# RWKV-7 chunks without transitions of their own, on one Trainium2 core

## The chip, the cores and the metric

The kernel runs on one core of a Trainium2 chip, in one launch. The metric is device time in microseconds (us), the median of several runs. Below, PE is the matmul engine (TensorE), DVE is VectorE, ACT is ScalarE, POOL is GpSimd and SP issues most DMAs. All data are float32; the large projections split each operand into a high and a low part of a shorter float format and add three products of those.

## The reference, cut to what matters

A two-layer trunk step over 640 tokens (512 latent, 128 context). Layer 1 has, beside another mixer, a bidirectional RWKV-7 mixer: 8 heads of width 64, each with a 64x64 state that is updated token by token, forwards and backwards.

```
def rwkv_direction(r, w, kk, a, v, kt, s0, reverse):
    def step(state, inp):
        r_t, w_t, kk_t, a_t, v_t, k_t = inp
        sa = jnp.einsum('bhvk,bhk->bhv', state, -kk_t)
        state = (state * w_t[:, :, None, :] + sa[..., None] * (kk_t * a_t)[:, :, None, :]
                 + v_t[..., None] * k_t[:, :, None, :])
        return state, jnp.einsum('bhvk,bhk->bhv', state, r_t)
    ...
    s_fin, o = lax.scan(step, s0, xs, reverse=reverse)
```

The kernel computes this in chunks of 64 tokens. Inside a chunk the vectors `sa` (called U) solve a triangular system: U = X (A S + K V), where S is the state at the chunk's start, X the inverse of a unit triangle made from the chunk's keys, A the decayed keys and K V the part that the chunk's own values give. The next state is decay x (S + B' U + K' V).

## The kernel before, in words

The RWKV work is cut into 8 units: 4 pairs of heads times 2 directions (`t = 2 p + d`). A unit has 10 chunks of 64 tokens: 8 of the latent sequence, one after the other, and 2 of the context sequence. The two heads of a pair lie on partitions 0 to 63 and 64 to 127 (`HS`; `KS` is the crossed order). Each unit passes three stages, each a Python generator in `rwkv`:

- `stage_a` (L1396) loads five operand arrays through `load`, multiplies them with the decays into `ar` (right sides A and receptance R) and `bk` (left sides), and forms the Gram products `gram`, masked on DVE into `gx` (L1444). The transposed left sides go to `gx` as well, the transposed values to `UV`.
- `stage_b` (L1475) inverts the triangle: 15 small DVE steps on 16x16 blocks, a trip through DRAM, then block merges with 32x32 products in the PSUM tag `pw`. After that it forms, for all ten chunks of both heads, what no state is needed for: it copies A and K V into `az`, multiplies both with the inverse (L1561), and multiplies the result once more with the left sides (`back`, L1546), which makes of every chunk a 64x64 transition matrix (in `ar[..., 0]`), a corrected right side (`ar[..., 1]`) and an own contribution (`UV`).
- `stage_c` (L1572) walks over the chunks. One link per chunk: two products of each head add up in one PSUM tile `HN` (L1606 to L1609: own contribution, and transition times state), ACT scales head 0's half and DVE head 1's half into the next state `hst` (L1612, L1613). `outputs` (L1585) forms the outputs of four chunks at a time in the tag `pz` (tile `O`).

The order is not written out by hand. In round `t` of the loop at L1651, `in_turn` deals out steps (`yield`s) of three streams in proportion to the counts that it is given: one stream with `finish`, then `stage_c` of unit t-2, then `stage_a` of unit t; one with `stage_b` of unit t-1; one with `FILL[t]` steps of the other mixer and of the projections (tiles `g` and `m`). A list scheduler then sets the final order of each engine from the dependencies, free buffers and times that it assumes. Each engine takes its own list strictly in order. PSUM has two buffers for `pw` and one for `pz`.

Of the kernel before, what the change touches and what calls it, by code (L numbers as in the profile page):

```python
# [291 lines left out]
class Trunk:  # L292
# [821 lines left out]
    def inputs(self, p, mix):  # L1114
# [31 lines left out]
        nc.vector.tensor_tensor(bb, bb, kk, op=ALU.mult)  # L1146
# [3 lines left out]
        nc.sync.dma_start(self.sp[p, 1], r)  # L1150
# [200 lines left out]
    def rwkv(self, other, most, more):  # L1351
# [44 lines left out]
        def stage_a(t, u):  # L1396
# [21 lines left out]
            kk = cl(rev(load(p, 0)))  # L1418
            nc.vector.tensor_scalar(ar[:, :, 0, 0:1], kk[:, :, 0:1], -1.0, None, op0=ALU.mult)
            nc.vector.scalar_tensor_tensor(ar[:, :, 0, 1:], kk[:, :, 1:], -1.0, e[:, :, :L - 1], op0=ALU.mult, op1=ALU.mult)  # L1420
            nc.vector.tensor_tensor(ar[:, :, 1, :], cl(rev(load(p, 1))), e, op=ALU.mult)
# [5 lines left out]
            gx = op.tile([P, 2, NCH, 3, L], F32, tag="gx", bufs=2, name="gx")  # L1427
            gA = gx[:, :, :, 0]
            UV = op.tile([P, 2, NCH, L], F32, tag="UV", bufs=2, name="UV")
# [8 lines left out]
            for c0, n in groups:  # L1438
                pss = [self.pt(tag, [P, 4, 2, L], "gram") for tag in ("pg", "pz")]
                for i in range(n):  # L1440
                    for h, hs in enumerate(HS):
                        self.mm(pss[h][:, i], fl(bk[hs, c0 + i]), fl(ar[hs, c0 + i]))
                for h in range(2):
                    nc.vector.tensor_tensor(gx[:, h, c0:c0 + n, 0:2], pss[h][:, :n], mg[:, :n], op=ALU.mult)  # L1444
                    yield
            for h, hs in enumerate(HS):
                nc.sync.dma_start(scr[h], gA[hs, h])
# [10 lines left out]
            for c0, n in groups:  # L1458
                ps = self.pt("pg", [P, 4, 2, L])
                for i in range(n):  # L1460
                    self.tr(fl(ps[:, i]), fl(bk[:, c0 + i]), ident)
                nc.scalar.copy(gx[:, :, c0:c0 + n, 2, :].rearrange("p h c l -> p c h l"), ps[:, :n])
                yield
            for c0 in range(0, NCH, 5):
                ps = self.pt("pg", [P, 5, L])
                for i in range(5):
                    for h, hs in enumerate(HS):
                        self.mm(ps[KS[h], i, :], vs[hs, (c0 + i) * L:(c0 + i + 1) * L], ident[hs, hs])
                for h, ks in enumerate(KS):
                    nc.scalar.copy(UV[ks, h, c0:c0 + 5, :], ps[ks])  # L1470
                yield

        def stage_b(t, u):


            ar, gA, gx, UV, sd = [u[n] for n in ("ar", "gA", "gx", "UV", "sd")]
# [27 lines left out]
            az = op.tile([P, NCH, 2, L], F32, tag="az", name="az")  # L1504
            for c0, n in ((0, 8), (8, 2)):
                for j in range(2):
                    ps = self.pt("pw", [P, 8, L])
                    for i in range(n):
                        for h, hs in enumerate(HS):
                            if j == 0:  # L1510
                                self.mm(ps[hs, i, :], ar[hs, c0 + i, 0, :], ident[hs, hs])
                            else:
                                self.mm(ps[hs, i, :], gA[KS[h], h, c0 + i, :], UV[KS[h], h, c0 + i, :])
                    (nc.vector.tensor_copy if j else nc.scalar.copy)(az[:, c0:c0 + n, j, :], ps[:, :n])
                    yield
# [14 lines left out]
            for i in range(NCH):  # L1530
                for h in range(2):
                    self.mm(ps[R4[2 * h + 1], i, :], gA[R4[2 * h], h, i, 32:64], xp[R4[2 * h], i, :])
# [7 lines left out]
            for h in range(2):  # L1540
                r0, r1 = R4[2 * h], R4[2 * h + 1]
                nc.vector.tensor_copy(gA[r0, h, :, 32:64], ps[r0])
                nc.scalar.copy(gA[r0, h, :, 0:32], xt[r0])
                nc.scalar.copy(gA[r1, h, :, 32:64], xt[r1])
            yield
            wts = []  # L1546

            def back(w4, c0, n):
                cs = slice(c0, c0 + n)
                ps = self.pt("pw", [P, 4, 2, L])  # L1550
                for i in range(n):
                    for h, hs in enumerate(HS):
# [4 lines left out]
            for c0, n in groups:  # L1557
                ps = self.pt("pw", [P, 4, 2, L])
                for i in range(n):
                    for h, hs in enumerate(HS):  # L1560
                        self.mm(ps[hs, i], gA[hs, h, c0 + i, :], az[hs, c0 + i])  # L1561
                w4 = op.tile([P, 4, L], F32, tag="w4", bufs=2, name="w4")
                nc.scalar.copy(w4[:, :n], ps[:, :n, 0, :])
                for h, hs in enumerate(HS):
                    nc.scalar.copy(UV[hs, h, c0:c0 + n, :], ps[hs, :n, 1, :])
                wts.append((w4, c0, n))
                yield
                if c0:
                    back(*wts.pop(0))
                    yield  # L1570
            back(*wts.pop(0))

        def stage_c(t, u):


            p, d = divmod(t, 2)
            ar, gx, UV, dec = [u[n] for n in ("ar", "gx", "UV", "dec")]
# [7 lines left out]
            def outputs(c0, n):  # L1585
                O = self.pt("pz", [P, 4, L], "O")
                for i in range(n):
                    Hc = st[c0 + i]
                    if Hc is not None:
                        for h, hs in enumerate(HS):  # L1590
                            self.mm(O[hs, i, :], Hc[:, h, :], ar[:, c0 + i, 1, :], start=True, stop=False)
                    for h, hs in enumerate(HS):
                        self.mm(O[hs, i, :], UV[:, h, c0 + i, :], gx[:, h, c0 + i, 1, :], start=Hc is None, stop=True)
# [6 lines left out]
            for s, n in [(1, 0), (0, 0), (1, 1), (0, 1)] + [(1, n) for n in range(2, 8)]:  # L1600
                ch = n + ((2 if d else 0) if s else (0 if d else 8))
                Hc = st[ch] = H[s]
                if s == 0 or n < 7:
                    HN = self.pt("pz", [P, L], "HN")
                    for h, hs in enumerate(HS):
                        self.mm(HN[hs], gx[:, h, ch, 2, :], UV[:, h, ch, :], start=True, stop=Hc is None)  # L1606
                    if Hc is not None:
                        for h, hs in enumerate(HS):
# [47 lines left out]
        for t in range(11):  # L1656
# [70 lines left out]
```

## Time and profile before

| | us |
|---|---|
| median of 3 runs (lowest, highest) | 2183.33 (2182.89, 2183.53) |
| profiled execution, whole | 2182.15 |
| profiled execution, span from first to last instruction | 2180.4 |
| stretch with the RWKV units, from the span's start | about 1040 to 1665 |

The profile lists, for each engine, what it did and what ended its idle time. A matmul of the program in plain float32 appears as two records, a projection's as one. Records of PE overlap in time, so the pace of a kind of product is read from one start to the next and not from its duration. Forms such as 128*64 give the part of PE's array that a product uses (rows*columns); 128*128 is all of it.

### The profile page before, as it was taken

The numbers are of one execution on the slowest core, as the hardware profiler recorded it, in microseconds if no ns is written. First come the engines' busy times: TensorE is split into PE (matmuls) and PEld (weight loads), VectorE is DVE, ScalarE is ACT, GpSimd is POOL, SyncE is SP. The second block draws the span as 40 slices with busy tenths as digits, with TensorE's granted clock in tenths as the row PEclk, the third lists the DMA queues.
The fourth block names the chain that finished last, engine by engine and source line by source line (L and its number), as shares of the span: only waits on it lengthen the run. The fifth ranks groups of instructions, "written<-read, shape, count | busy, mean of one in ns | idle before, by whom it ended". The sixth has DMA issues, their size and how long they took to land.

```text
span 2180.4 us, 44790 instructions
## 1 busy us (share of the span) xinstructions
PE 2080.5 (95%) x18461; PEld 1895.1 (87%) x18461; DVE 1349.3 (62%) x3067; ACT 1018.6 (47%) x2072; POOL 0.2 (0%) x4
## 2 busy tenths in 40 slices
PE   7899989999999999999999999898989999999997
PEld 5896778888899999989888788786777999999997
DVE  3858686557636647746774755745567674574663
ACT  4645464455414515546655545544344552452551
POOL 0000000000000000000000000000000000000000
PEclk9899999999999999999999999998989999999999
DMA  7114420125525222332542242332312222222212
GB/s 295 60 46 151 141 66 25 44 99 205 205 86 183 67 79 78 109 106 72 167 117 81 74 118 83 97 100 84 94 31 61 76 70 78 78 66 81 74 62 89
DMA packets 138061, 212.50 MB, mean 97 GB/s; under 512 B 51456, under 2 KB 68736, under 8 KB 131712
## 3 DMA queue, kind: packets, MB, share of 16 engines
q1 hardware_dynamic: 131168, 205.56, 29.2%
q10 hardware_dynamic: 6688, 4.07, 0.6%
q8 instruction: 145, 2.38, 0.5%
q14 instruction: 60, 0.49, 0.1%
HBM read 187.49 MB, written 22.09 MB: 96 GB/s over the span
## 4 chain that ended last, share of the span: by engine, by line
PE 85%; DVE 7%; DMA 4%; ACT 3%; issue 1%; SPq 0%; ACTq 0%; DVEq 0%
PE e L331 46%; PE g L331 21%; PE m L331 5%; PE pw L331 4%; PE S L331 3%; PE m L334 2%; DMA wa<-in_adaw 1%; PE gram L331 1%; PE pg L331 1%; PE HN L331 1%; PE O L331 1%; DMA in<-sp 1%; DVE wl L578 0%; ACT pr L768 0%; PE pg L334 0%
## 5 line engine op out<-in xcount | busy, mean ns | idle before, releaser
L331 PE MATMUL e<-hi,wh 128*128 128x320 f32 (+1 forms) x2240 | 693.4, 312 | 3.2 <-ACT hi L511 1.8
L331 PE MATMUL e<-lo,wh 128*128 128x320 f32 (+1 forms) x2240 | 695.5, 311 | 0.1
L331 PE MATMUL e<-hi,wl 128*128 128x320 f32 (+1 forms) x2240 | 691.3, 310 | 2.1 <-DVE wl L578 2.1
L577 ACT CAST wh<-wr 128x512 fp32r<-128x512 f32 (+3 forms) x434 | 237.6, 586 | 519.8 <-PE e L331 385.2
L331 PEld LDWEIGHTS e<-hi,wh 128*128 128x128 f32 x2240 | 421.4, 189 | 19.6 <-ACT tg L965 7.5
L331 PEld LDWEIGHTS e<-hi,wl 128*128 128x128 f32 x2240 | 422.9, 189 | 8.6 <-DVE wl L578 3.6
L331 PEld LDWEIGHTS e<-lo,wh 128*128 128x128 f32 x2240 | 422.5, 189 | 1.3 <-DVE lo L513 1.3
L578 DVE TENSOR_TENSOR wl<-wr,wh 128x512 fp32r<-128x512 f32 (+3 forms) x434 | 267.7, 647 | 74.5 <-ACT wh L577 73.9
L331 PE MATMUL g<-hi,wh 128*128 128x320 f32 (+1 forms) x928 | 302.9, 327 | 3.9 <-DVE x L625 1.3
L331 PE MATMUL g<-lo,wh 128*128 128x320 f32 (+1 forms) x928 | 296.0, 319 | 1.3 <-DVE lo L475 1.3
L331 PE MATMUL g<-hi,wl 128*128 128x320 f32 (+1 forms) x928 | 296.2, 319 | 0.0
L331 PEld LDWEIGHTS g<-hi,wh 128*128 128x128 f32 x928 | 178.4, 193 | 14.2 <-issue 2.2
L331 PEld LDWEIGHTS g<-lo,wh 128*128 128x128 f32 x928 | 178.3, 192 | 5.4 <-DVE lo L475 1.8
L331 PEld LDWEIGHTS g<-hi,wl 128*128 128x128 f32 x928 | 178.3, 192 | 2.5 <-issue 1.0
L625 DVE SCALAR_TENSOR_TENSOR x<-e,mod,x 128x320 f32<-128x320 f32 x168 | 67.0, 437 | 139.6 <-PE e L331 139.4
L966 ACT ACTIVATE tu<-tu,bias 128x512 f32<-128x512 f32 (+1 forms) x176 | 88.6, 548 | 0.0
L553 DVE TENSOR_SCALAR bias<-e 128x2 f32<-128x2 f32 x95 | 15.2, 159 | 117.1 <-PE e L331 117.1
L768 ACT ACTIVATE pr<-S,nm 128x768 f32<-128x768 f32 (+1 forms) x80 | 63.7, 797 | 47.5 <-DVE nm L766 28.1
L766 DVE TENSOR_REDUCE nm<-S 128x1 f32<-128x768 f32 (+1 forms) x80 | 65.1, 820 | 17.5 <-PE S L331 16.9
L976 ACT ACTIVATE tg<-tg 128x640 f32<-128x640 f32 x44 | 32.5, 739 | 79.9 <-DVE tg L943 79.9
L554 DVE TENSOR_TENSOR tu<-e,rstd 128x320 f32<-128x320 f32 x86 | 41.8, 488 | 38.3 <-PE e L331 38.2
L331 PE MATMUL g<-wa,csT 128*32 128x512 f32 x352 | 49.5, 635 | 12.1 <-DMA wa<-in_adaw 12.0
(398 smaller groups left out, 2914.5 us busy)
## 6 DMA issues: line engine op xcount, KB each, us to landing
wa<-in_adaw SPq DMA_DIRECT2D x48, 1024.0 KB
wr<-in_wup SPq DMA_DIRECT2D x176, 256.0 KB
wr<-in_wod SPq DMA_DIRECT2D x70, 256.0 KB
wr<-in_wdn SPq DMA_DIRECT2D x64, 256.0 KB
in<-sp SPq DMA_DIRECT2D x42, 320.0 KB
wr<-in_wev SPq DMA_DIRECT2D x36, 256.0 KB
wr<-in_wdn SPq DMA_DIRECT2D x32, 192.0 KB
x<-in_xT SPq DMA_DIRECT2D x8, 320.0 KB
```

The costliest lines, as they stand in the source:

```text
L331: self.nc.tensor.matmul(out, lhsT, rhs, start=start, stop=stop)
L334: self.nc.tensor.transpose(out, in_, ident)
L553: nc.vector.tensor_scalar(bias, p1[:, HT:], scale, None, op0=ALU.mult)
L554: nc.vector.tensor_tensor(t[:, :HT], p0, self.rs[:, :HT], op=ALU.mult)
L577: nc.scalar.copy(wh[:, a:b, :], wr)
L578: nc.vector.tensor_tensor(wl[:, a:b, :], wr, wh[:, a:b, :].bitcast(F32), op=ALU.subtract)
L625: nc.vector.scalar_tensor_tensor(o, ps, gate[:, m, s:s + 1], o, op0=ALU.mult, op1=ALU.add)
L766: nc.vector.tensor_reduce(nm[:, m:m + 1], S[m], AX.XY, ALU.max, negate=True)
L768: nc.scalar.activation(t[:, :nb * w].rearrange("p (b w) -> p b w", b=nb), S[m], AF.Exp, bias=nm[:, m:m + 1], accum_out=st[:, m:m + 1])
L966: nc.scalar.activation(u[:, a:b], u[:, a:b], AF.Identity, bias=b0[:, s:s + 1])
L976: nc.scalar.activation(gt, gt, AF.Silu)
```

## The change

`stage_b` ends with the inverse; the transitions, the corrected right sides, `az` and `back` go. K V alone is kept (`kv`). The off-diagonal blocks of the inverse's array are cleared on GpSimd, so that both heads' inverses stand in one 128x128 block-diagonal operand `gA`. The layouts of `gx`, `UV` and `ar` are turned so that a chunk's data of both heads lie side by side; in `ar`, the A of head 0 stands beside the R of head 1, and `inputs` writes the arrays to DRAM in that crossed order, with the sign already in them. `stage_c` then has, per chunk, three products over the whole array in one PSUM tile `Y`: the right sides Y = A S, to which DVE adds `kv` (`z`); U = `gA` z, copied into `UV` by ACT for head 0 and by DVE for head 1; N = left sides times U and V, from which DVE makes the two halves of the next state, with the old state scaled by ACT beforehand (`hd`). `outputs` moves from the tag `pz` to `pw`. The counts that `in_turn` is given become 31 for `stage_c`, 13 for `stage_a` and 8 for `stage_b` (13, 15 and 17 before).

```
 # inputs
-            nc.vector.tensor_tensor(kk[:, hs], kk[:, hs], ps, op=ALU.mult)
-        nc.sync.dma_start(self.sp[p, 0], kk)
+            nc.vector.scalar_tensor_tensor(kk[:, hs], kk[:, hs], -1.0, ps, op0=ALU.mult, op1=ALU.mult)
+        nc.sync.dma_start(self.sp[p, 0, h0], kk[h0])
+        nc.sync.dma_start(self.sp[p, 1, h1], kk[h1])
...
 # stage_a
+            for i in range(2):
+                s = cl(rev(load(p, i)))
+                ha, hr = HS[i], HS[1 - i]
+                nc.scalar.copy(ar[ha, :, i, 0:1], s[ha, :, 0:1])
+                nc.vector.tensor_tensor(ar[ha, :, i, 1:], s[ha, :, 1:], e[ha, :, :L - 1], op=ALU.mult)
+                nc.vector.tensor_tensor(ar[hr, :, i, :], s[hr], e[hr], op=ALU.mult)
...
-                    nc.vector.tensor_tensor(gx[:, h, c0:c0 + n, 0:2], pss[h][:, :n], mg[:, :n], op=ALU.mult)
+                    for i in range(2):
+                        nc.vector.tensor_tensor(gx[:, i, c0:c0 + n, h], pss[h][:, :n, i ^ h], mg[:, :n, i], op=ALU.mult)
...
 # stage_b
-                                self.mm(ps[hs, i, :], ar[hs, c0 + i, 0, :], ident[hs, hs])
...
+                nc.scalar.copy(kv[:, c0:c0 + n], ps[:, :n])
+            for h in range(2):
+                nc.gpsimd.memset(gA[KS[h], :, h, :], 0.0)
...
-                        self.mm(ps[hs, i], w4[hs, i, :], gx[hs, h, c0 + i, 1:3])
-                nc.vector.tensor_tensor(ar[:, cs, 0, :], ps[:, :n, 1, :], i64.unsqueeze(1).broadcast_to([P, n, L]), op=ALU.add)
-                nc.vector.tensor_tensor(ar[:, cs, 1, :], ps[:, :n, 0, :], ar[:, cs, 1, :], op=ALU.add)
...
-                        self.mm(ps[hs, i], gA[hs, h, c0 + i, :], az[hs, c0 + i])
...
 # stage_c
-                O = self.pt("pz", [P, 4, L], "O")
+                O = self.pt("pw", [P, 4, L], "O")
...
-                    HN = self.pt("pz", [P, L], "HN")
-                        self.mm(HN[hs], gx[:, h, ch, 2, :], UV[:, h, ch, :], start=True, stop=Hc is None)
-                            self.mm(HN[hs], ar[:, ch, 0, :], Hc[:, h, :], start=False, stop=True)
-                    nc.scalar.activation(H[s][HS[0], 0], HN[HS[0]], AF.Copy, scale=dec[HS[0], ch:ch + 1])
-                    nc.vector.tensor_scalar(H[s][HS[1], 1], HN[HS[1]], dec[HS[1], ch:ch + 1], None, op0=ALU.mult)
+                y = self.pt("pz", [P, 512], "Y")
+                    self.mm(Y, fl(ar[:, ch]), fl(Hc))
+                        nc.vector.tensor_tensor(z[hs], Y[hs, h * L:(h + 1) * L], kv[hs, ch], op=ALU.add)
+                self.mm(U, fl(gA[:, ch]), z)
+                    (nc.vector.tensor_copy if h else nc.scalar.copy)(UV[hs, ch, h, :], U[hs])
+                    self.mm(N, fl(gx[:, 2, ch]), fl(UV[:, ch]))
+                        nc.scalar.activation(hd, Hc, AF.Copy, scale=dec[:, ch:ch + 1])
+                            nc.vector.scalar_tensor_tensor(H[s][hs, h], N[hs, h * L:(h + 1) * L], dec[hs, ch:ch + 1], hd[hs, h],
+                                                           op0=ALU.mult, op1=ALU.add)
...
-                n += 13
+                n += 31
-                n += 15
+                n += 13
-                streams.append((stage_b(t - 1, U[t - 1]), 17))
+                streams.append((stage_b(t - 1, U[t - 1]), 8))
```

The lists that the scheduler makes of both kernels show what moves. First PE's list inside the third round, while projections (`g`) are there to run. Before, the links of the first unit's chunks stand as one block (two products from `UV` and `gx`, two from the state `hst` and `ar`):

```order
L331 MATMUL pw_12397<-UV_11362,gx_11361 64x64 [waits DVE_49]
L331 MATMUL pw_12397<-UV_11362,gx_11361 64x64
L331 MATMUL HN_12263<-UV_10905,gx_10904 64x64 [waits DVE_49]
L331 MATMUL HN_12263<-UV_10905,gx_10904 64x64
L331 MATMUL HN_12263<-hst4_10843,ar_10887 64x64 x2
L331 MATMUL pw_12397<-UV_11362,gx_11361 64x64 x2
L331 MATMUL g_12418<-hi0_10278,wh_12408 128x320
```

In the changed kernel, at the same place, an N product (`Y_12147` from `UV` and `gx`) and single output products `O`, one per head:

```order
L331 MATMUL g_12415<-lo2_10288,wh_12404 128x320
L331 MATMUL O_12202<-gx_10909,UV_10910 64x64 [waits Activation_49]
L331 MATMUL g_12415<-hi2_10280,wl_12405 128x320
L331 MATMUL Y_12147<-UV_10910,gx_10909 128x128 [waits DVE_49]
L331 MATMUL O_12202<-gx_10909,UV_10910 64x64
L331 MATMUL g_12415<-hi3_10281,wh_12404 128x320
```

The block of four is gone; the outputs no longer stand in groups of sixteen but come one product at a time, each where its head's U is there.

Second, PE's list near the end of the last unit's `stage_c`. Before (the `m` are the other mixer's last products):

```order
L331 MATMUL HN_18514<-UV_17163,gx_17162 64x64 [waits DVE_49]
L331 MATMUL HN_18514<-UV_17163,gx_17162 64x64
L331 MATMUL HN_18514<-hst3_10842,ar_17145 64x64 x2
L331 MATMUL HN_18532<-UV_17163,gx_17162 64x64 [waits DVE_49]
L331 MATMUL HN_18532<-UV_17163,gx_17162 64x64
L331 MATMUL HN_18532<-hst4_10843,ar_17145 64x64 x2
L331 MATMUL m_18506<-on32_95,hsq_18497 128x1 [waits PE_49,Activation_49]
```

In the changed kernel, one whole chunk and the start of the next (`Y` from `hst` and `ar` is A S, `Y` from `z` is U, `Y` from `UV` is N):

```order
L331 MATMUL Y_18313<-hst1_10842,ar_17069 128x128 [waits DVE_49,PE_49]
L331 MATMUL Y_18313<-z_18315,gx_17089 128x64 [waits DVE_49]
L331 MATMUL O_18433<-gx_17089,UV_17090 64x64 [waits Activation_49]
L331 MATMUL Y_18313<-UV_17090,gx_17089 128x128 [waits DVE_49]
L331 MATMUL O_18433<-gx_17089,UV_17090 64x64
L331 MATMUL O_18433<-ar_17069,hst3_10844 64x64 [waits DVE_49]
L331 MATMUL Y_18349<-hst3_10844,ar_17069 128x128 [waits DVE_49,PE_49]
L331 MATMUL O_18433<-ar_17069,hst3_10844 64x64
```

Where a chunk had one wait for DVE, it has three, and nothing stands between the three products but single outputs of the same chunk.

Third, DVE's list while the first unit's `stage_c` runs, late chunks of it. Before, a chunk's share is one instruction (`hst` from `HN`):

```order
L1613 TENSOR_SCALAR hst6_10845<-HN_12346,dec_10902 64x64 [waits Activation_49]
L1423 TENSOR_TENSOR bk_12540<-in_12541,cs_12474 128x10x64 [waits Activation_49]
L578 TENSOR_TENSOR wl_12756<-wr_12757,wh_12755 128x512 [waits DVE_49,DMAHW2_49,PE_49,Activation_49]
L578 TENSOR_TENSOR wl_12756<-wr_12761,wh_12755 128x512 [waits DMAHW3_49,Activation_49]
L1613 TENSOR_SCALAR hst7_10846<-HN_12371,dec_10902 64x64 [waits Activation_49]
```

In the changed kernel, the share of one chunk (two `z`, the copy to `UV`, two `hst`) among instructions of the other mixer (`hk`, `hac`, `hq`) and of `inputs` (`kk`, `bb`):

```order
L1587 TENSOR_TENSOR z_12526<-Y_12524,kv_11577 64x64 [waits PE_49]
L1587 TENSOR_TENSOR z_12526<-Y_12524,kv_11577 64x64
L1144 SCALAR_TENSOR_TENSOR kk_12925<-kk_12925,m_13047 128x384 [waits PE_49]
L1144 SCALAR_TENSOR_TENSOR kk_12925<-kk_12925,m_13051 128x256 [waits PE_49]
L1147 SCALAR_TENSOR_TENSOR bb_12929<-bb_12929,kk_12925 128x640 [waits DVE_49]
L1592 COPY UV_10910<-Y_12524 64x64 [waits Activation_49]
L1251 COPY_PREDICATED hac_12615<-lev_9774,m_13094 128x160 [waits PE_49]
L1288 TENSOR_TENSOR hq_11964<-hq_11964,hf_11962 128x40x2x8
L1603 SCALAR_TENSOR_TENSOR hst0_10841<-Y_12524,dec_10907,hd_12566 64x64 [waits PE_49]
L1603 SCALAR_TENSOR_TENSOR hst0_10841<-Y_12524,dec_10907,hd_12566 64x64
```

One instruction per chunk becomes five in three places, with longer instructions queued between the places.

## Rows read from the trace of the kernel before

**Rows 1.** The page: busy time, and the chain that ended last by engine.
```profile
PE 2080.5 (95%) x18461; PEld 1895.1 (87%) x18461; DVE 1349.3 (62%) x3067; ACT 1018.6 (47%) x2072; POOL 0.2 (0%) x4
...
PE 85%; DVE 7%; DMA 4%; ACT 3%; issue 1%; SPq 0%; ACTq 0%; DVEq 0%
```

**Rows 2.** Busy time by stretch: the whole stage, then three DVE-heavy parts of it.
```profile
core 0: us, PE busy (x) PEld busy (x) DVE busy (x) ACT busy (x) POOL busy (x), PEclk, DMA share, GB/s
1040.00:1665.00 625.00, 584.49 (x8334) 506.37 (x8332) 386.28 (x958) 294.78 (x653) 0.00 (x0) 0.93 0.32 94
1080.00:1110.00 30.00, 25.16 (x436) 21.96 (x437) 27.47 (x74) 18.77 (x39) 0.00 (x0) 0.77 0.49 140
1210.00:1240.00 30.00, 25.55 (x521) 21.73 (x520) 25.86 (x74) 20.91 (x45) 0.00 (x0) 0.92 0.34 93
1360.00:1400.00 40.00, 33.56 (x549) 29.62 (x548) 31.59 (x84) 21.31 (x52) 0.00 (x0) 0.87 0.34 87
```

**Rows 3.** Timeline: one link of the last unit with nothing else on PE.
```profile
1639.58 0.34 PE L331 MATMUL HN<-UV,gx 128*64 128x64 f32 x4
...
1640.14 0.31 ACT L1612 ACTIVATE hst<-HN,dec 64x64 f32<-64x64 f32 x1
...
1640.48 0.29 DVE L1613 TENSOR_SCALAR hst<-HN,dec 64x64 f32<-64x64 f32 x1 [3.73 <-ACT hst L1612]
...
1640.83 0.34 PE L331 MATMUL HN<-UV,gx 128*64 128x64 f32 x4 [0.80 <-DVE hst L1613]
```

**Rows 4.** Who waited for the state `hst` in the stage (us, times).
```profile
  PE HN L331: 8.5, 8
...
  PE O L331: 5.0, 5
```

**Rows 5.** Chain in order of time (start, us, what): 64x64 products, then outputs.
```profile
1127.96 1.02 PE pw L331 x16
...
1129.63 0.73 PE pg L331 x20
...
1183.88 1.08 PE O L331 x32
```

**Rows 6.** Timeline of PE: full-array float32 products of the other mixer.
```profile
1637.03 0.39 PE L331 MATMUL m<-hq,hk 128*128 128x128 f32 x2
1637.25 0.39 PE L331 MATMUL m<-hat,hvt 128*128 128x128 f32 x2
...
1641.21 1.27 PE L331 MATMUL m<-on,hsq 128*128 128x1 f32 x10
```

**Rows 7.** Timeline of PE: one link's four products among projections.
```profile
1151.74 0.31 PE L331 MATMUL g<-hi,wl 128*128 128x320 f32 x1
...
1151.89 0.31 PE L331 MATMUL g<-hi,wh 128*128 128x320 f32 x1
...
1152.13 0.34 PE L331 MATMUL HN<-UV,gx 128*64 128x64 f32 x4
...
1152.51 0.42 PE L331 MATMUL g<-lo,wh 128*128 128x320 f32 x1
...
1152.77 0.31 PE L331 MATMUL g<-hi,wl 128*128 128x320 f32 x1
```

**Rows 8.** Groups of DVE instructions in the stage, by form (count, busy us, mean ns).
```profile
L1613 DVE TENSOR_SCALAR hst<-HN,dec 64x64 f32<-64x64 f32 x72 | 20.9, 291 | 47.8 <-ACT hst L1612 46.2
L1444 DVE TENSOR_TENSOR gx<-gram,conT 128x512 f32<-128x512 f32 x32 | 20.8, 686 | 19.3 <-PE gram L331 19.3
...
L1554 DVE TENSOR_TENSOR ar<-pw,i 128x256 f32<-128x256 f32 x16 | 6.8, 423 | 9.6 <-PE pw L331 9.5
...
L1421 DVE TENSOR_TENSOR ar<-in,lw 128x640 f32<-128x640 f32 x8 | 6.6, 819 | 0.0
...
L1554 DVE TENSOR_TENSOR ar<-pw,i 128x128 f32<-128x128 f32 x8 | 2.3, 286 | 0.6 <-PE pw L331 0.6
```

More of the change, by code (lines that the diff above doesn't have):

```diff
@@ L1149, in inputs @@
         r = yield from mix(i + 1, "rr")
-        nc.sync.dma_start(self.sp[p, 1], r)
+        nc.sync.dma_start(self.sp[p, 1, h0], r[h0])
+        nc.sync.dma_start(self.sp[p, 0, h1], r[h1])
         nc.vector.scalar_tensor_tensor(kt, r, self.par("rkw", p), kt, op0=ALU.mult, op1=ALU.mult)
@@ L1426, in stage_a @@
             nc.vector.tensor_copy(dec, e[:, :, L - 1])
-            gx = op.tile([P, 2, NCH, 3, L], F32, tag="gx", bufs=2, name="gx")
-            gA = gx[:, :, :, 0]
-            UV = op.tile([P, 2, NCH, L], F32, tag="UV", bufs=2, name="UV")
+            gx = op.tile([P, 3, NCH, 2, L], F32, tag="gx", bufs=2, name="gx")
+            gA = gx[:, 0]
+            UV = op.tile([P, NCH, 2, L], F32, tag="UV", bufs=2, name="UV")
             vs = load(p, 4)
@@ L1461, in stage_a @@
                     self.tr(fl(ps[:, i]), fl(bk[:, c0 + i]), ident)
-                nc.scalar.copy(gx[:, :, c0:c0 + n, 2, :].rearrange("p h c l -> p c h l"), ps[:, :n])
+                nc.scalar.copy(gx[:, 2, c0:c0 + n], ps[:, :n])
                 yield
@@ L1469, in stage_a @@
                 for h, ks in enumerate(KS):
-                    nc.scalar.copy(UV[ks, h, c0:c0 + 5, :], ps[ks])
+                    nc.scalar.copy(UV[ks, c0:c0 + 5, h, :], ps[ks])
                 yield
         def stage_b(t, u):
-            ar, gA, gx, UV, sd = [u[n] for n in ("ar", "gA", "gx", "UV", "sd")]
+            gA, UV, sd = [u[n] for n in ("gA", "UV", "sd")]
             mt, sb = mts[t % 2], scb[t % 2]
@@ L1503, in stage_b @@
             nc.vector.transpose(fl(xp), fl(xt))
-            az = op.tile([P, NCH, 2, L], F32, tag="az", name="az")
+            kv = u["kv"] = op.tile([P, NCH, L], F32, tag="kv", bufs=2, name="kv")
             for c0, n in ((0, 8), (8, 2)):
[L1506 to L1510, printed above, removed]
-                                self.mm(ps[hs, i, :], ar[hs, c0 + i, 0, :], ident[hs, hs])
[L1512 to L1515, printed above, removed]
+                ps = self.pt("pw", [P, 8, L])
+                for i in range(n):
+                    for h, hs in enumerate(HS):
+                        self.mm(ps[hs, i, :], gA[KS[h], c0 + i, h, :], UV[KS[h], c0 + i, h, :])
+                nc.scalar.copy(kv[:, c0:c0 + n], ps[:, :n])
+            for h in range(2):
+                nc.gpsimd.memset(gA[KS[h], :, h, :], 0.0)
+            yield
             ps = self.pt("pw", [P, NCH, 32])
@@ L1541, in stage_b @@
                 r0, r1 = R4[2 * h], R4[2 * h + 1]
[L1542 to L1552, printed above, removed]
-                        self.mm(ps[hs, i], w4[hs, i, :], gx[hs, h, c0 + i, 1:3])
-                nc.vector.tensor_tensor(ar[:, cs, 0, :], ps[:, :n, 1, :], i64.unsqueeze(1).broadcast_to([P, n, L]), op=ALU.add)
-                nc.vector.tensor_tensor(ar[:, cs, 1, :], ps[:, :n, 0, :], ar[:, cs, 1, :], op=ALU.add)
[L1557 to L1560, printed above, removed]
-                        self.mm(ps[hs, i], gA[hs, h, c0 + i, :], az[hs, c0 + i])
[L1562 to L1571, printed above, removed]
+                nc.vector.tensor_copy(gA[r0, :, h, 32:64], ps[r0])
+                nc.scalar.copy(gA[r0, :, h, 0:32], xt[r0])
+                nc.scalar.copy(gA[r1, :, h, 32:64], xt[r1])
         def stage_c(t, u):
             p, d = divmod(t, 2)
-            ar, gx, UV, dec = [u[n] for n in ("ar", "gx", "UV", "dec")]
+            ar, gA, gx, UV, dec, kv = [u[n] for n in ("ar", "gA", "gx", "UV", "dec", "kv")]
             if d == 0:
@@ L1590, in outputs @@
                         for h, hs in enumerate(HS):
-                            self.mm(O[hs, i, :], Hc[:, h, :], ar[:, c0 + i, 1, :], start=True, stop=False)
+                            self.mm(O[hs, i, :], Hc[:, h, :], ar[:, c0 + i, 1 - h, :], start=True, stop=False)
                     for h, hs in enumerate(HS):
-                        self.mm(O[hs, i, :], UV[:, h, c0 + i, :], gx[:, h, c0 + i, 1, :], start=Hc is None, stop=True)
+                        self.mm(O[hs, i, :], UV[:, c0 + i, h, :], gx[:, 1, c0 + i, h, :], start=Hc is None, stop=True)
                 if d == 0:
```

29 lines of the change are left out of this document (19 added, 10 removed).

## The prediction

> **What bounds the kernel now.** I read the page first, then the busy time by stretch, then the timeline around single links, then the groups of DVE. The page gives PE 95% busy and 85% of the chain that ended last [rows 1], so a reader's first thought is that fewer PE products mean less time. The stretches correct this. The change lies inside one stage of 625 us, where PE is busy 584 us, DVE 386 us and ACT 295 us [rows 2]. PE is the tightest there, but its 584 us hold waits that are not visible as idle time, because records overlap, and 41 us are idle outright. In three stretches of together 100 us, a sixth of the stage, DVE is busy 85 of 100 us and PE only 84 of 100 [rows 2]: there DVE leads. All other layers are untouched, and I take them as unchanged.
>
> The recurrence itself is a chain: PE, ACT, DVE, PE. With nothing else on PE it takes 1.25 us per chunk (products at 1639.58, the next at 1640.83), and PE stood still for 0.80 us of that [rows 3]. Over the whole stage the state made PE wait only 8.5 us before `HN` and 5.0 us before `O` [rows 4], 13.5 us for 72 links: nearly every link is covered by projections. So the question is whether longer links stay covered.
>
> **PE's products.** Records per kind are counted in PE's lists, two per float32 product. Removed are 640 records of 64x64 products with 128 columns, at 1.02/16 = 0.064 us each (40.8 us), 320 with 64 columns at 0.73/20 = 0.037 us (11.7 us), and the 544 records of `HN` at the pace of the outputs of the same form, 1.08/32 = 0.034 us (18.4 us) [rows 5]: 70.9 us. Added are 72 Y, 80 U and 72 N, all over the full array. A full-array product with 128 columns takes 1637.25 - 1637.03 = 0.22 us, and one with a single column still 1.27/10 x 2 = 0.25 us [rows 6], so U with its 64 columns is no cheaper: 224 x 0.22 = 49.3 us. Net -22 us (-31 us if U took half; +16 us at the other end, if every one cost its whole 0.39 us from start to end [rows 6]).
>
> **Changes of tiling.** A block of four `HN` products between projections takes 1152.77 - 1151.89 = 0.88 us including two projection steps of 0.15 us [rows 7], so 0.58 us, of which 8 x 0.034 = 0.27 us is its own pace. The visit to a smaller tiling costs the other 0.31 us. Such visits rise from 176 to 268 by the lists, although Y, U and N need none: `O` no longer comes sixteen products at a time but one by one. 92 x 0.31 = 28 us at most. Many lone `O` stand beside a wait that PE has anyway, where the visit costs nothing; I take half, +14 us (range 0 to 28).
>
> **The waits.** A chunk now has three links. DVE's additions and copies of 64 columns from PSUM do not occur before; two points, 286 ns for 128 columns and 423 ns for 256 [rows 8], give an estimate of 0.22 us, and the state's scaling with its per-partition factor is 0.29 us at exactly this size. With the hops of 0.06 us to and from PE and 0.03 us from ACT to DVE of [rows 3], and 0.39 us for a product from start to end [rows 6]: Y to U is 0.39 + 0.06 + 2 x 0.22 + 0.06 = 0.95 us; U to N is 0.39 + 0.06 + 0.31 (ACT) + 0.03 + 0.22 + 0.06 = 1.07 us (DVE's copy waits for ACT's by the list, as `hst` does now); N to the next Y is 0.39 + 0.06 + 2 x 0.29 + 0.06 = 1.09 us. Together 3.11 us per chunk for 1.25 us. All of a unit's chunks share the one `pz` buffer, so context and latent chunks cannot overlap. Queued behind a waiting product on PE is everything: projections, Gram products, the inverse of the next unit.
>
> What covers these links is read from the changed PE list. In 20 of 72 cases U stands directly behind its Y with at most a lone `O` between, in 17 of 72 N behind U, in 19 of 71 the next Y behind N; before, only 4 of 71 links stood so. Less the 0.22 us that PE works itself, that is 20 x 0.73 + 17 x 0.85 + 19 x 0.87 = 46 us of standing still. These 56 places are not spread evenly: they are the ends of the rounds, and the last unit's chunks almost as a whole, since nothing is left to deal out there. The same reckoning for before gives 4 x 0.98 = 4 us against the 13.5 us observed, so 9.6 us or 0.135 us per link came on top, from instructions queued ahead on DVE; 215 links of that size are 29 us. Upper bound 46 + 29 - 13.5 = +62 us, middle 46 - 13.5 = +32 us; if all of it fell on PE time that is idle now (41 - 13.5 us), +5 us. I take +45 us, nearer to the observed kind of link than to the bare one, less some that falls on idle time.
>
> **DVE.** Per unit it gains 18 `z` and 10 copies at 0.22, 18 state updates at 0.29, 6 more and shorter masks (8 x 0.423 + 4 x 0.286 for 4 x 0.686 + 2 x 0.423: +0.9), and two more multiplications of 0.82 into `ar`; it loses 9 `hst` at 0.29, six additions (2.3), and the copies of `az` (0.686 + 0.286) [rows 8]. Net +8 us, 64 us in all. Beside PE this is free wherever DVE has room; in the DVE-led sixth of the stage it is on the path, about a sixth, 10 us. Some is in the 0.135 us above already: I take +9 us (0 to 21, a third).
>
> The Trainium skill's page "Perfetto Trace Analysis", section "Optimizing Scalar/DVE Operations", gives a fixed engine-busy cost of about 125 ns for a DVE access to PSUM. An estimate from that page, with 69 ns for 64 columns, is 0.19 us for each small operation, which would make DVE's gain 44 us instead of 64. The measured 0.29 us of `hst` decides for its own kind; the other kinds are not in the trace.
>
> **Costed at nothing.** ACT loses 9 `hst` and the copies of `pw`, gains 10 copies and 8 scalings of like size: even, and it is half idle. The two GpSimd memsets per unit (64x640) are not shown; the nearest row is DVE's 0.82 us for 640 columns. They stand between K V and the last write of the inverse, with several block products between; uncovered they would be about 8 x 2 x 0.8 = 13 us at most, and no less than nothing. SP issues three to four more half-size writes per pair, whose data are read a round later.
>
> **Sum.** -22 + 14 + 45 + 9 = +46 us on the profiled execution's 2182.15 us (span 2180.4 and 1.75 around it): 2228 us; the median of the runs lies 1.2 us above that execution, so 2229 us.
>
> **Rivals.**
> - Faster. The waits stay covered because the scheduler fills with what it has, the new visits fall into idle time, and only the work counts: -22 us, 2161 us. For it speaks PE's 85% of the chain [rows 1] and that before only 13.5 us of link waits showed [rows 4]; against it the 56 bare places in the list. It decides if fewer than about a third of those places cost anything. The Trainium skill's "Perfetto Trace Analysis", section "Matmuls", says that larger matmuls are more efficient than smaller ones when possible, which is this rival's mechanism. Chance 0.15.
> - No change: waits of about +3 us cancel the work after tilings and DVE are paid. Chance 0.07.
> - Much slower. DVE is the new bound: it answers late at all 215 links and not only at the bare ones, waits at +62, visits +28, a third of DVE's gain on the path (+21): -22 + 62 + 28 + 21 = +89 us, 2272 us. For it speaks DVE's 85% in three stretches [rows 2], against it the 62% over the stage. Chance 0.23.
> - My forecast, +46 us with an own range of 2205 to 2253 us: 0.55.
>
> **Numbers.** About 0.2%, 4.4 us, is what a measurement of this kernel can tell from no change. Faster 0.15, same 0.07, slower 0.78. The range 2176 to 2285 us reaches past the much slower case and down into no change, and leaves out most of the faster case.
>
> **What would show it.** PE should have about 1060 fewer records (1504 gone, 448 new). The stage should take some 670 us instead of 625, with DVE's busy time near 450 us. Waits of PE for `z`, `UV` and `hst` together should be 50 to 75 us, most of them at the ends of rounds and in the last unit, whose `stage_c` should take about 3 us per chunk. If PE's waits for these stay under 20 us, the forecast is wrong at that step; if the time grows while they stay small, DVE or a DMA is late elsewhere.

## The result, and the profile after

The changed kernel takes 2337.98 us (2335.53 to 2340.81) against 2183.11: ratio 1.071, 95% interval 1.0693 to 1.0728. It is slower, as forecast, but by 155 us and not by 46, and past the range's upper end of 2285. The page of the changed kernel, answering [rows 1], with the granted clock in 40 slices:

```profile
PE 2204.8 (94%) x17405; PEld 1986.0 (85%) x17405; DVE 1418.5 (61%) x3355; ACT 1015.9 (43%) x2086; POOL 10.2 (0%) x20
...
PEclk9899989999999999999989898555767899999999
...
PE 85%; DVE 7%; ACT 4%; DMA 3%; issue 1%; SPq 0%; ACTq 0%; DVEq 0%
```

The shares hardly differ from before: the page alone tells nothing. The clock's row does: a hole of nine slices. Busy time by stretch of the changed kernel, with the columns of [rows 2], first the whole stage (it ends at 1825.8 instead of 1667.9):

```profile
1040.00:1826.00 786.00, 709.19 (x7281) 597.42 (x7279) 456.90 (x1251) 292.28 (x668) 10.01 (x16) 0.78 0.26 75
1300.00:1440.00 140.00, 134.28 (x1505) 118.62 (x1503) 88.92 (x224) 65.49 (x144) 1.25 (x2) 0.91 0.31 93
1440.00:1628.00 188.00, 156.76 (x1233) 119.58 (x1233) 91.19 (x294) 46.72 (x118) 3.75 (x6) 0.51 0.21 52
1690.00:1826.00 136.00, 119.98 (x1113) 94.37 (x1111) 77.18 (x219) 35.98 (x94) 1.25 (x2) 0.70 0.10 28
```

From 1440 to 1628 us PE is busy 83% at half clock (1.2 GHz). What is missing there is seen in the same view for the instructions on `wh` alone, two thirds of the projections that cover the links (stretches from one unit's first Gram product to the next one's). Before:

```profile
1264.00:1356.00 92.00, 47.02 (x197) 32.74 (x197) 7.83 (x12) 6.84 (x12) 1.00 0.34 98
1356.00:1419.00 63.00, 18.96 (x75) 13.12 (x75) 4.02 (x6) 3.42 (x6) 0.92 0.35 97
1419.00:1506.00 87.00, 37.01 (x148) 25.68 (x148) 5.41 (x10) 4.73 (x10) 0.93 0.32 97
1506.00:1550.00 44.00, 9.82 (x40) 7.32 (x40) 0.89 (x2) 0.82 (x2) 0.70 0.32 86
```

After:

```profile
1227.00:1336.00 109.00, 58.77 (x250) 41.78 (x250) 10.33 (x16) 9.10 (x16) 0.97 0.29 86
1336.00:1446.00 110.00, 53.27 (x208) 36.51 (x208) 7.02 (x12) 6.18 (x12) 0.90 0.33 96
1446.00:1514.00 68.00, 0.00 (x0) 0.00 (x0) 0.00 (x0) 0.00 (x0) 0.50 0.16 39
1514.00:1592.00 78.00, 1.98 (x4) 1.16 (x4) 0.90 (x2) 0.82 (x2) 0.50 0.21 55
```

The cover is spent by 1446 us. How it goes: the timeline of one covered link, answering [rows 7]. `z` is ready at 1152.34, and U starts at 1155.58, behind 21 projections (19 of them started after `z` was ready) and a block product that the order on PE had put into this wait:

```profile
1151.88 0.46 DVE L1587 TENSOR_TENSOR z<-Y,kv 64x64 f32<-64x64 f32 x2 [2.57 <-PE Y L331]
1152.03 0.42 PE L331 MATMUL g<-hi,wh 128*128 128x320 f32 x1
...
1155.09 0.31 PE L331 MATMUL g<-hi,wl 128*128 128x320 f32 x1
1155.33 0.32 PE L331 MATMUL pw<-UV,gx 64*64 64x64 f32 x2
1155.58 0.43 PE L331 MATMUL Y<-z,gx 128*128 128x64 f32 x2
```

And a bare chunk of the last unit at half clock, answering [rows 3]: 4.32 us from Y to Y where 3.11 were reckoned.

```profile
1802.87 0.79 PE L331 MATMUL Y<-hst,ar 128*128 128x128 f32 x2
...
1803.70 0.46 DVE L1587 TENSOR_TENSOR z<-Y,kv 64x64 f32<-64x64 f32 x2 [0.52 <-PE Y L331]
1804.21 0.69 PE L331 MATMUL Y<-z,gx 128*128 128x64 f32 x2
1804.94 0.21 ACT L1592 COPY UV<-Y 64x64 f32<-64x64 f32 x1 [1.72 <-PE Y L331]
1805.18 0.23 DVE L1592 COPY UV<-Y 64x64 f32<-64x64 f32 x1 [1.02 <-ACT UV L1592]
...
1805.61 0.80 PE L331 MATMUL Y<-UV,gx 128*128 128x128 f32 x2
...
1806.44 0.60 DVE L1603 SCALAR_TENSOR_TENSOR hst<-Y,dec,hd 64x64 f32<-64x64 f32 x2 [1.03 <-PE Y L331]
...
1807.19 0.79 PE L331 MATMUL Y<-hst,ar 128*128 128x128 f32 x2
```

PE's waits in the stage for the three links' operands (waiter, releaser, us, times, longest), answering [rows 4], are 33 us in all, the smallest left out here:

```profile
PE O L331 <- DVE UV L1592: 11.8, 5, 3.2
...
PE O L331 <- ACT UV L1592: 7.7, 25, 0.7
...
PE Y L331 <- DVE z L1587: 5.1, 11, 0.6
...
PE Y L331 <- DVE hst L1603: 3.7, 2, 1.9
PE Y L331 <- DVE UV L1592: 3.6, 7, 0.7
```

The groups of VectorE and of PE by form (count, busy us, mean ns), answering [rows 8] and [rows 5, 6]: the small VectorE operations cost what was reckoned (0.29 us for `hst`, 0.22 for `z` and for the copy to `UV`); PE's means are over both levels of the clock.

```profile
L1603 DVE SCALAR_TENSOR_TENSOR hst<-Y,dec,hd 64x64 f32<-64x64 f32 x128 | 36.2, 283 | 54.7 <-PE Y L331 52.5
L1587 DVE TENSOR_TENSOR z<-Y,kv 64x64 f32<-64x64 f32 x144 | 31.9, 222 | 54.2 <-PE Y L331 52.4
...
L1592 DVE COPY UV<-Y 64x64 f32<-64x64 f32 x80 | 18.2, 228 | 53.0 <-ACT UV L1592 51.6
```

```profile
L331 PE MATMUL O<-gx,UV 128*64 128x64 f32 x320 | 56.3, 288 | 19.6 <-DVE UV L1592 11.8 <-ACT UV L1592 7.7
...
L331 PE MATMUL Y<-hst,ar 128*128 128x128 f32 x128 | 39.9, 404 | 4.2 <-DVE hst L1603 3.7
L331 PE MATMUL Y<-z,gx 128*128 128x64 f32 x144 | 36.8, 349 | 6.6 <-DVE z L1587 5.1
```

So the time is not mainly in waits that can be seen, nor in a slow VectorE. The stage splits into three parts: PE's idle time (no record running); the records at full pace (for each kind, by the tile that it writes, its count times its mean distance to the next record's start at full clock, idle taken off); and the rest, put down to the half clock. Worked out so from the traces, in us:

| kernel | time | stage | idle | records at full pace | half clock's cost | time at half clock |
|---|---|---|---|---|---|---|
| before | 2183 | 628 | 42 | 562 | 24 | 82 |
| changed | 2338 | 786 | 76 | 574 | 136 | 348 |
| cover held in its round | 2352 | 794 | 88 | 591 | 115 | 345 |
| cover in sixes, tied | 2315 | 754 | 87 | 573 | 94 | 239 |
| warm products added | 2356 | 807 | 80 | 659 | 68 | 209 |
| two waits per chunk | 2288 | 733 | 76 | 554 | 103 | 282 |
| one wait per chunk | 2261 | 703 | 71 | 563 | 70 | 197 |
| before, three waits | 2353 | 795 | 110 | 603 | 81 | 280 |
| before, outputs apart | 2149 | 591 | 28 | 555 | 7 | 27 |

The stage's 158 us are 34 of idle time, 12 of work and 112 of half clock. The split is an accounting: with kinds divided more finely (by the operands too) it comes to 10 to 15 of work and 109 to 114 of half clock, and a single row moves by up to 23. Some 10 of the 112 are time in which a product before a wait still shows as running. The experiments ask what causes it.

PE's order shows how the cover is spread: projection records ahead of each of the 28 products of a unit's chain, second and fourth unit of the changed kernel.

```
47 19 21 9 0 0 5 18 14 21 17 16 4 17 22 22 19 22 19 10 19 21 12 10 0 0 0 0
0 0 0 0 0 0 0 0 0 0 0 0 0 0 0 0 0 0 0 0 0 0 0 0 0 0 0 0
```

A wait of some 1.0 us, three times a chunk, is filled with up to 3 us of projections as long as there are any, and later with none. Over all eight units, 136 of the 224 products of the chain have no projection ahead of them, and 109 of these run at half clock.

### The profile page after: what moved, and what is told of

It reads as the page before. It is cut to its first block, busy times and chain, and to the rows that moved or that the text cites. A ratio compares the mean times of both kernels' runs of the same rounds, so it can differ in the third digit from the quotient of the medians.

```text
span 2338.8 us, 43185 instructions
## 1 busy us (share of the span) xinstructions
PE 2204.8 (94%) x17405; PEld 1986.0 (85%) x17405; DVE 1418.5 (61%) x3355; ACT 1015.9 (43%) x2086; POOL 10.2 (0%) x20
## 4 chain that ended last, share of the span: by engine, by line
PE 85%; DVE 7%; ACT 4%; DMA 3%; issue 1%; SPq 0%; ACTq 0%; DVEq 0%
PE e L331 43%; PE g L331 19%; PE m L331 5%; PE Y L331 4%; PE O L331 3%; PE S L331 3%; PE pw L331 2%; PE pg L331 2%; PE m L334 2%; PE gram L331 2%; DMA wa<-in_adaw 2%; DMA in<-sp 1%; PE pg L334 1%; DVE z L1587 0%; ACT pr L768 0%
## 5 line engine op out<-in xcount | busy, mean ns | idle before, releaser
L331 PE MATMUL O<-gx,UV 128*64 128x64 f32 x320 | 56.3, 288 | 19.6 <-DVE UV L1592 11.8
L331 PEld LDWEIGHTS O<-gx,UV 128*64 128x64 f32 x320 | 35.1, 170 | 41.1 <-DVE UV L1592 12.7
L1603 DVE SCALAR_TENSOR_TENSOR hst<-Y,dec,hd 64x64 f32<-64x64 f32 x128 | 36.2, 283 | 54.7 <-PE Y L331 52.5
```

The source lines that it names most:

```text
L331: self.nc.tensor.matmul(out, lhsT, rhs, start=start, stop=stop)
L1603: nc.vector.scalar_tensor_tensor(H[s][hs, h], N[hs, h * L:(h + 1) * L], dec[hs, ch:ch + 1], hd[hs, h], op0=ALU.mult, op1=ALU.add)
```

## The experiments

The first theories were A (the cover was drawn forward, and the empty rounds cost), B (the links' own length costs) and C (PE's work grew). When A had failed, D (coarse cover) and E (the number of waits in series, which B had as their length) joined C, and later E' (that number, by way of bare rounds at half clock).

**Cover held in its round.** The dealt projections may be issued on PE only behind the last product of the round before:

```
-  streams.append((part(other, FILL[t]), FILL[t]))
+  streams.append((self.held(other, FILL[t], self.last.ins), FILL[t]))
```

> The changed kernel with one thing added: the covering products that are dealt in round t are issued on PE only behind the last product of round t-1 (an order edge, no wait, no instruction more or less). Theory A (the cover was pulled forward: the profile of the changed kernel has 1040 projection records in its first four rounds and 6 in the next two, where the granted clock is 0.50 from 1443 to 1628 us): most of the loss in rounds 5 to 7 goes, 60 to 120 us off 2338, so 2220 to 2280, with the clock of the stage back above 0.85. Theory B (the links' own length sets the time, three waits per chunk wherever the cover stands): no round gains, since the early ones lose the cover that the late ones get: 2320 to 2350. Theory C (PE's work itself grew, by more visits to another tiling): 2320 to 2350 as well, but with a clock above 0.85.

2352.12 us, ratio 1.0773 (1.0750 to 1.0795). Theory A, that the cover's being drawn forward is the price, falls: now every round from 1199 us on has a bare end at half clock instead of rounds 5 and 6. The bare places were moved, not filled: 345 us at half clock for 348.

**Cover spent early in the kernel before.** `FILL = 25, 46, 46, 45, 40, 0, 0, 0`.

> The kernel before with only the numbers that deal the cover changed (25, 46, 46, 45, 40, 0, 0, 0 for 19, 25, 30, 31, 30, 29, 19, 19), so that rounds 5 to 7 have as few projections (6 float32 product pairs) as the changed kernel's have. Theory A (bare rounds are the price, whatever the links' form): slower by 40 to 100 us, 2220 to 2280, with a granted clock near 0.5 in the bare rounds. Theory B (the new links alone are slow, the old ones with one wait are not): less than 20 us, 2183 to 2203, and the clock above 0.8 there. Theory C (work): within 5 us of 2183.

2240.65 us, 1.0259 (1.0239 to 1.0279). Bare rounds do cost the old links, 57 us; over a third of what the change lost. The clock was 0.68 in the barest 100 us (1500 to 1600), not near 0.5.

**No chain from chunk to chunk.** `Hc = st[ch] = u["st0"]` where a state existed, with the first experiment's edges.

> The changed kernel with the order edges of the first experiment, and with each chunk's right side, state and output taken from the unit's first state instead of the state that the chunk before it left: same products, same copies, no wait from one chunk to the next (the chain from state to state is left out, so that the numbers are those of another recurrence). What is left over 2183 is then the price of the products and copies themselves. Theory A and theory B: 2175 to 2200 (my sum had -22 for products and +14 for visits; the records at full clock in the two traces say +10). Theory C (PE's work grew): 2250 or more.

2329.60 us, 1.0664 (1.0642 to 1.0686). It didn't take away what it meant to: Y, U and N of all chunks still share one bank, and in the trace a chunk's first product still follows the last chunk's state update. As a price of the products it is void.

**Warm products.** `for i in range(k): self.mm(y[:, 3 * P:], ident, ident)`, with k = 3, behind Y, U and N in three units.

> The changed kernel, order of the cover untouched, with three full-array float32 products of the identity by itself put on PE straight behind each of the three products of a chunk in the units of rounds 5 to 7 (252 products more, 56 us of PE at full clock by 0.22 us each; nobody reads them). Theory A1 (in the bare rounds it is the half clock that costs, and PE's idle time brings it): the clock of 1443 to 1628 us comes up to 0.8 or more, the added products stand in waits, and the time does not rise, or falls to 2290 to 2335. Theory A2 (the waits cost, the clock is only a sign of them): added products that stand in waits cost nothing and those that don't cost up to 56 us at full or 112 us at half clock: 2340 to 2430, clock still near 0.5 or, where it rises, no gain.

2355.56 us, 1.0786 (1.0757 to 1.0815). Where the changed kernel had 0.51, the row now reads:

```profile
1450.00:1686.00 236.00, 195.57 (x2117) 165.32 (x2119) 106.29 (x341) 55.41 (x139) 3.75 (x6) 0.88 0.19 48
```

The clock rose with the added products, as A1 said, but the time is outside A1's range and inside A2's, which had foreseen a rising clock without gain. By the table the half clock costs 68 us less and the records 85 us more, while idle time stayed (80 us for 76). So the added work did not go into idle time that shows, as A2 has it; that 85 us of work raised the time by only 18 speaks for the clock's cost being real, but does not show it.

**Every piece of cover tied to its place**, in the changed kernel and then in the one before:

```
+  with self.tc.issue_after(self.last.ins):   # at each piece, not at each round
+      next(g, None)
```

> The changed kernel with its cover (projections and the other head's work, rounds 0 to 10) tied on PE to the place where it is dealt: each dealt piece is issued only behind the last product that stands ahead of it in the program (order edges, same instructions). In PE's order of the changed kernel a chunk's wait holds 10 to 25 projection records in the first half of a round and none in the other half or in rounds 5 to 7; here it holds 0 or 12, alternating, to a round's end. Theory D (the cover is piled into some waits and missing in others, so that PE works past the end of the wait in the first and idles, at half clock, in the second): 2200 to 2290, half-clock time of the stage down from 355 us to under 200. Theory E (28 waits in series per unit are the bound wherever the cover stands): 2330 to 2370. Theory C (PE's work grew): no change, 2330 to 2350.

2323.80 us, 1.0638 (1.0614 to 1.0663): 14 us back where theory D had 50 to 140; nearer to E. The half clock's time did fall, from 348 to 232 us (D: under 200), but PE's idle time rose from 76 to 97: less time at half clock did not bring the time back by itself.

> The kernel before with the same ties. Theory D: its waits are a third as many, and each has cover already, so little changes: 2170 to 2210. Theory C and theory E say the same; the run is the control that the ties by themselves cost or bring nothing.

2202.36 us, 1.0090 (1.0069 to 1.0111): the ties cost the kernel before 20 us, so they are not neutral, and may hide as much of a gain in the run ahead of it.

**Two waits, first try.** `self.mm(N, fl(gx[:, 2, ch]), fl(UV[:, ch]) if Hc is None else fl(zz))`, z written twice.

> The changed kernel with the state's addition taken straight from the right sides z (written twice side by side) instead of from the inverse's product UV, which is still made and copied for the outputs: two waits in series per chunk in place of three, same products, one DVE instruction of 128 instead of 64 columns (the recurrence computed is another one). Theory E (the number of waits in series is the bound): the chain of 8.6 us per chunk falls by about a third, 2338 - 80 x 2.0 to 2.9 = 2105 to 2180, no lower than the work allows, so 2180 to 2230. Theory D (placing of the cover): a third of the waits less to cover, 2270 to 2310. Theory C (work): 2330 to 2340.

2343.05 us, 1.0734 (1.0716 to 1.0752), a miss by construction: in its trace the addition still begins after UV's copies, in all 64 chunks. The next run puts it ahead of them.

**Two waits, then one.**

```
   self.mm(N, fl(gx[:, 2, ch]), fl(zz))      # one wait: fl(Hc), beside Y
   ...                                       # hst from N
   self.mm(U, fl(gA[:, ch]), z)              # inverse and copies behind
```

> The changed kernel with two waits per chunk: as in the run before (the addition takes the right sides z, so another recurrence is computed), but now the addition's product stands on PE ahead of the inverse's, and the state's two updates ahead of the inverse's copies, so that the chain no longer passes the inverse; in the run before it still did, by the order on PE and DVE. Products and copies as many as in the changed kernel. Theory E' (each further wait in series per chunk draws cover out of the later rounds, leaves them bare, and the bare rounds run at half clock): half of what is lost beyond the work comes back, 2250 to 2285; half-clock time of the stage 180 to 260 us instead of 355. Theory C (full-array products and visits to other tilings): 2325 to 2345.

2287.92 us, 1.0472 (1.0447 to 1.0497): 50 us back, at the same products and copies. Theory C falls. E' is just missed: 2288 us where 2250 to 2285 were expected, and 282 us at half clock for 180 to 260.

> The same with one wait per chunk: the addition's product takes the state itself and stands beside the right sides' product (another recurrence again), and the addition's columns of the bank alternate between chunks; right sides, inverse and copies are made as in the changed kernel, but for the outputs alone, off the chain. Theory E': nearly all comes back but the work: 2190 to 2230, half-clock time 90 to 150 us. Theory C: 2320 to 2345.

2260.93 us, 1.0356 (1.0325 to 1.0386): 77 us back, though less than expected (197 us at half clock for 90 to 150). In its trace the next Y of a unit still starts behind UV's copies of the chunk before, in all 64 places and 1.8 us later on the mean, so the inverse was off the data's chain but not out of the order. What holds the remaining 78 us is open. The stage with two waits, then with one:

```profile
1040.00:1773.00 733.00, 656.61 (x7285) 567.38 (x7284) 463.47 (x1251) 289.77 (x669) 10.01 (x16) 0.81 0.29 80
```

```profile
1040.00:1743.00 703.00, 631.68 (x7283) 544.75 (x7281) 463.59 (x1251) 290.61 (x668) 10.02 (x16) 0.86 0.29 83
```

**The kernel before with three waits.** Between two chunks, twice:

```
+                            self.mm(y[:, i * P:(i + 1) * P], ident, fl(Hc))
...
+                                (nc.vector.tensor_copy if h else nc.scalar.copy)(hc[hs], y[hs, i * P:(i + 1) * P].rearrange("p (h l) -> p h l", l=L))
```

> The kernel before with two waits more per chunk and nothing else of the change: the state goes twice through PE (a product with the identity, 128x128) and a copy (half by ScalarE, half by VectorE) before the next chunk uses it; 128 full-array products more (256 records, 28 us by 0.11), a ring of seven states instead of eight, and the cover dealt over the longer stream. Theory E': as slow as the changed kernel or slower, 2310 to 2370, with cover gone from rounds 5 and 6 and a half clock there. Theory C: the products' 28 us and the bare waits, 2210 to 2250.

2352.92 us, 1.0778 (1.0749 to 1.0808). This is the run that decides: none of the change's products, tilings or masks, and the loss is there, 170 us. What it adds are two waits in series with what makes them, 128 products and their copies; the count that `in_turn` is given for `stage_c` is 29 instead of 13. By the table the stage's 167 us are 68 of idle time, 41 of work and 57 of half clock, so by this the products themselves are about a quarter. The stage and a middle stretch of this kernel, then its `wh` alone in nearly the same stretch:

```profile
1040.00:1835.00 795.00, 684.36 (x8592) 586.84 (x8590) 433.03 (x1091) 324.63 (x780) 0.00 (x0) 0.82 0.26 74
...
1440.00:1660.00 220.00, 169.30 (x2065) 136.18 (x2065) 92.15 (x270) 66.08 (x179) 0.00 (x0) 0.62 0.19 49
```

```profile
1442.00:1640.00 198.00, 7.02 (x18) 5.06 (x18) 0.87 (x2) 0.81 (x2) 0.59 0.19 50
```

The same picture as in the changed kernel: cover gone, half clock.

**Shorter waits, as many.** Both halves of UV copied by VectorE in the changed kernel; both halves of the state scaled by VectorE in the one before.

> The changed kernel with both halves of UV copied by VectorE, where ScalarE took the first. In its trace the two copies take 0.97 us from first start to last end (80 times), because the second begins after the first; two on VectorE would take 0.46 us by its own 0.23 us. The waits stay as many, each chunk is 0.5 us shorter. If the length of the bare waits sets the time (80 chunks, of which 40 to 50 stand bare): 15 to 40 us less, 2298 to 2323. If it is the number of waits that draws the cover out of the later rounds, and not their length: 2325 to 2340; PE's order holds as many projections per round as before.

2334.49 us, 1.0695 (1.0677 to 1.0713): 4 us for 0.5 us less in each of 80 chunks (the two copies take 0.48 us in its trace, 0.99 in the changed kernel's), and the interval overlaps the changed kernel's. The length of this one hop hardly counts here.

> The kernel before with both halves of the state scaled by VectorE, where ScalarE took the first: the one wait that its chunks have becomes 0.2 to 0.3 us shorter of 1.25 (0.31 on ScalarE and then 0.29 on VectorE, against two of 0.29). If the few bare waits matter (13.5 us waited for the state before): 3 to 15 us faster, 2168 to 2180. If they are covered: 2180 to 2186.

2169.10 us, 0.9933 (0.9912 to 0.9954): 15 us faster than before, as expected if the few bare waits matter. Here a shorter wait did pay, with as many waits, so the run above does not show that length never counts.

**Cover in sixes.** Still open by then was whether fair cover would hide three waits. A projection yields after every second of its eight steps instead of every fourth, each piece tied, `FILL = 12, 16, 24, 30, 30, 30, 30, 30`.

> The changed kernel with its cover cut into pieces of 6 projection records in place of 12, each tied on PE to its place behind the chain's products, and dealt 12, 16, 24, 30, 30, 30, 30, 30 over the rounds, so that nearly every wait of the first six units holds 6 or 12 records (0.9 or 1.8 us) and few hold none; same instructions. If the three waits cost only because the cover is heaped (10 to 25 records in some waits, none in others): 2200 to 2280, half-clock time of the stage under 150 us. If it is their number in series, which a fair cover cannot hide, since PE then stands on cover when the operand is ready: 2300 to 2350.

2315.06 us, 1.0609 (1.0586 to 1.0631). Two thirds of the waits of the first six units (111 of 168 by the trace) now hold 6 or more records, against 60 in the changed kernel; 23 us come back, no more. Cover as fair as this doesn't hide three waits in series. It was not as fair as meant (57 of the 168 hold none), and the ties cost 20 us in the kernel before, so what wholly even cover would bring is not shown.

**Outputs apart.** The last kernel before with `O = self.pt("pw", [P, 4, L], "O")`.

> The kernel before with the state scaled by VectorE alone, as in the last run of it, and with the outputs O in the banks of pw, as the changed kernel has them, so that a chunk's state product does not wait for an output group to leave its bank. If outputs in the chain's bank cost some waits: 2 to 12 us under the 2169 of that run. If pw's two banks are needed by stage_b: 2170 to 2185.

2149.34 us, 0.9854 (0.9831 to 0.9878): faster than both kernels, by 33 us than before, and by more than the 2 to 12 us expected on the run with VectorE alone. Its stage and its clock:

```profile
1040.00:1631.00 591.00, 562.74 (x8325) 489.27 (x8324) 399.48 (x1029) 277.99 (x583) 0.00 (x0) 0.98 0.35 99
```

```profile
PEclk9899999999999999999999999999999999999999
```

The Trainium skill's "Perfetto Trace Analysis", section "Matmuls", advises that independent groups rotate through different PSUM banks; this run agrees, with some 17 us between the two ratios. Time at half clock fell from 68 to 27 us between the two, so most of the gain need not be the waits for the bank themselves.

## Why the prediction missed

Its mechanism, longer links that the cover does not fill, was right. The step that failed is the term of the waits: it took 56 places of the order as bare, priced each as PE standing still for 0.73 to 0.87 us, took the other links at 0.135 us or nothing, and put the clock at nothing without a reason. The trace has 57 such places by the same rule, but 136 products of the chain with no projection ahead of them, 109 of them at half clock; and of the stage's 158 us only 34 are idle time, while the accounting puts 112 down to the half clock.

- **Products** (-22): right in the sum, by parts that offset each other. At full pace the block products fell by 58 us (forecast 52.5), `HN` by 29 (18.4), and Y, U, N cost 69 (49.3; 0.153 us per record): -18. Records fell by 1053 (forecast 1060).
- **Changes of tiling** (+14, at most 28): too small. The 608 records of `O`, now one by one, went from 0.036 to 0.098 us each at full pace: +38. Some of that can be the wait of the product behind a lone `O`. With what other kinds saved, the work in all is +12 where -8 was forecast.
- **Waits as standing still** (+45, between 5 and 62): idle time rose by 34, right in size. PE's waits for `z`, `UV` and `hst` are 33 us, between the two signs that the forecast had named (50 to 75 if right, under 20 if wrong), and the stage took 786 us, not 670: the missing time is not in waits that the profile shows.
- **DVE** (+9): its busy time is 457 us, forecast 450, so the rival that made DVE the bound has no support: runs with 3, 2 and 1 waits have 457, 463 and 464 us of DVE and differ by 77 us.
- **Costed at nothing**: ACT 292 us for 295, GpSimd 10 us with no wait of PE on it. Right.
- **Missing: the clock**, +112 us by the accounting. The prediction's own list of PE showed bare places at the ends of rounds, and [rows 2] showed a granted clock of 0.77 in a stretch with gaps; the two were not put together. The full list would also have shown 6 projections in the rounds of two units, where before had 335.

Without the half clock's added cost the sum of measured terms is +46 us, the forecast's figure; that is luck, since its work was 20 us too low and its waits and DVE 20 us too high. That waits in series bring both the idle time and the half clock is shown by the kernel before with three of them (+170, of which 41 are work) and by the changed one with fewer (-50, -77). That the clock by itself costs 112 us is not shown apart from its cause, and 78 us of the loss stay with one wait.

The Trainium skill's "TensorE: Matmul & The Clock Gate", section "A second HAM failure mode: psum-queue depth-cycling", says that frequent short pauses of PE between groups of products make its clock swing between the two levels. This trace agrees in part: short pauses did go with a lost clock, but from 1443 to 1628 us it stayed at 0.5 without a swing, through 45 pauses of together 29 us, the longest 2.06 us. The Trainium skill's "TensorE: Matmul & The Clock Gate", section "Terms", makes the penalty of a clock at half rate about half of the time spent there; by that estimate 266 us more at half clock cost 133 us, where the accounting gives 112.

## What to carry to other kernels

Count the waits in series that a change adds to a recurrence before counting the products that it saves: with two more per chunk this kernel lost 155 and, in another form, 170 us, though PE's work grew by only 12 and 41. Read from the order how much independent work each wait and each round has left, and ask what the clock will be where there is none: by the accounting the half clock was 112 of the stage's 158 us, the idle time 34. In the kernel before, scaling the state on one engine instead of two and moving the outputs out of the chain's bank were worth 33 us without any new arithmetic.

## What was not expected of the hardware

That a more even cover helped so little: the time fell by 23 us, and PE still idled 87 us. And that 252 useless products raised the clock from 0.51 to 0.88 in the bare rounds for 18 us in all, though they are 85 us of records at full pace.
